# Rotary embedding on one core: a partition's DRAM run doubled from 16 KB to 32 KB, partitions interleaved from two batches

## The chip, the cores and the metric

The kernel runs on one core of a Trainium2 chip. The metric is the device time of one execution in microseconds (us). Runs are sorted into a fast and a slow state by time and granted clock; all timed runs quoted were in the fast state, and one single look has the state "unknown".

## The reference

```python
batch, seq, dim = (16, 512, 1024);  num_heads = 16      # head_dim 64, half 32
x1, x2 = x[..., :half_dim], x[..., half_dim:]           # per head
rotated = concatenate([x1 * cos - x2 * sin, x1 * sin + x2 * cos], axis=-1)   # cos, sin: [seq, 32]
```

Everything is float32. The input has 33.55 MB and so has the output. Each number is read once, used in two multiplications and an addition, and written once.

## The kernel before

A tile is one batch: 128 partitions with R = 4 rows each, 2 MB, and in DRAM one contiguous run of 16 KB for each partition. A ring of 40 rows (ten tiles) lives in SBUF, the core's on-chip memory. The sync engine's queue (SP) issues loads, the scalar engine's queue (ACT) issues stores. One row of a tile in all 128 partitions is a "unit" of work: VectorE multiplies by the cosines, GpSimd (for one unit in eight VectorE) multiplies the swapped halves by the sines, and VectorE, or TensorE with ScalarE, adds the two and writes back into the ring.

```python
R = 4;  RING = 40;  NC = batch
xv = x.rearrange("b (p r) d -> b p (r d)", r=R)
ov = out.rearrange("b (p r) h d -> b p (r h d)", r=R)

def on_sync(sp):
    for c in range(NC):
        if c * R >= RING:
            sp.wait_ge(sem_out[c - RING // R], 16)      # the slot's old tile has been stored
        sp.dma_start(tile(c), xv[c]).then_inc(sem_in[c], 16)
        if c == 0:
            ... # cos and sin tables: 128 partitions x 512 B each
# on_scalar, after the last unit of tile c:
    ae.dma_start(ov[c], tile(c)).then_inc(...)
```

Of the kernel before, what the change touches and what calls it, by code (L numbers as in the profile page):

```python
# [6 lines left out]
def bass_split_heads_rope_kernel(  # L7
# [14 lines left out]
    batch, seq, dim = x.shape  # L22
    H = int(num_heads)
    HD = dim // H
    HALF = HD // 2
    P = 128
    R = 4
    assert P * R == seq

    fp32 = mybir.dt.float32  # L30
    bf16 = mybir.dt.bfloat16
    mult = mybir.AluOpType.mult
# [1 line left out]
    COPY = mybir.ActivationFunctionType.Copy  # L34

    RING = 40
    NC = batch
    NU = batch * R

    def where(u):  # L40
        return u // R, u % R, u % RING


    PE2 = [u % 8 in (1, 3, 6) for u in range(NU)]
    V2 = [u % 8 == 3 for u in range(NU)]

    def count(flags):
        return [sum(flags[: u + 1]) for u in range(NU)]

    n_pool = count([not v for v in V2])  # L50
    n_dve = count(V2)
    n_pe = count(PE2)
# [3 lines left out]
    NT2 = 6  # L56
# [4 lines left out]
    with ExitStack() as stack:  # L61
        x_sb = stack.enter_context(nc.sbuf_tensor([P, RING, H, 2, HALF], fp32))
        t2_sb = stack.enter_context(nc.sbuf_tensor([P, NT2, H, 2, HALF], fp32))
        stage = stack.enter_context(nc.sbuf_tensor([P, 2, R * HALF], fp32))
        s_sb = stack.enter_context(nc.sbuf_tensor([P, R, 2, HALF], fp32))
        ident = stack.enter_context(nc.sbuf_tensor([P, P], fp32))
        zero = stack.enter_context(nc.sbuf_tensor([P, BANK], bf16))
        tab_ps = stack.enter_context(nc.psum_tensor([P, BANK], fp32))
        t1_ps = stack.enter_context(nc.psum_tensor([P, NT1, H * HD], fp32))
        sem_in = [stack.enter_context(nc.semaphore(f"in{c}")) for c in range(NC)]  # L70
        sem_out = [stack.enter_context(nc.semaphore(f"out{c}")) for c in range(NC - RING // R)]
        sem_rest = stack.enter_context(nc.semaphore("rest"))
        sem_cos = stack.enter_context(nc.semaphore("cos"))
        sem_sin = stack.enter_context(nc.semaphore("sin"))
        sem_c = stack.enter_context(nc.semaphore("ctab"))
# [9 lines left out]
        sem_a = stack.enter_context(nc.semaphore("act"))  # L85

        c_ps = tab_ps[:, 0:R * HALF].rearrange("p (r d) -> p r d", d=HALF)
        s_ps = tab_ps[:, R * HALF:R * (HALF + HD)].rearrange("p (r t d) -> p r t d", t=2, d=HALF)

        xv = x.rearrange("b (p r) d -> b p (r d)", r=R)  # L90
        ov = out.rearrange("b (p r) h d -> b p (r h d)", r=R)
        xs = x_sb[:].rearrange("p n h t d -> p n (h t d)")

        def tile(c):
            k = c * R % RING
            return x_sb[:, k:k + R].rearrange("p n h t d -> p (n h t d)")

        def swapped(k):
            return x_sb[:, k, :, ::-1, :]

        def sin_of(table, r):
            return table[:, r, None, :, :].broadcast_to([P, H, 2, HALF])

        def wait_added(eng, u):

            if n_pe[u]:
                eng.wait_ge(sem_a, n_pe[u])
            if n_comb[u]:
                eng.wait_ge(sem_v, n_comb[u])

        def wait_t2_free(eng, u):

            if u >= NT2:
                v = u - NT2
                if PE2[v]:
                    eng.wait_ge(sem_e, n_pe[v])  # L116
                else:
                    eng.wait_ge(sem_v, n_comb[v])

        def on_sync(sp):  # L120
            for c in range(NC):
                if c * R >= RING:
                    sp.wait_ge(sem_out[c - RING // R], 16)
                sp.dma_start(tile(c), xv[c]).then_inc(sem_in[c], 16)  # L124
                if c == 0:
                    for i, (table, sem) in enumerate(((cos, sem_cos), (sin, sem_sin))):
                        sp.dma_start(  # L127
                            stage[:, i, :], table.rearrange("(p r) d -> p (r d)", r=R)
                        ).then_inc(sem, 16)
            sp.wait_ge(sem_rest, 16 * (NC - len(sem_out)))  # L130

        def on_scalar(ae):
            ae.wait_ge(sem_sin, 16)
            sv = stage[:, 1, :].rearrange("s (r d) -> s r d", d=HALF)
            ae.activation(s_sb[:, :, 0, :], sv, COPY, scale=-1.0)  # L135
            ae.activation(s_sb[:, :, 1, :], sv, COPY).then_inc(sem_s, 1)  # L136
            for u in range(NU):
                c, r, k = where(u)
                if PE2[u]:
                    ae.wait_ge(sem_e, n_pe[u])  # L140
                    ae.activation(xs[:, k, :], t1_ps[:, u % NT1, :], COPY).then_inc(sem_a, 1)  # L141
                if r == R - 1:
                    wait_added(ae, u)
                    ae.dma_start(ov[c], tile(c)).then_inc(sem_out[c] if c < len(sem_out) else sem_rest, 16)

        def on_tensor(pe):
            pe.wait_ge(sem_z, 1)
# [5 lines left out]
            pe.wait_ge(sem_i, 2)  # L153
            for u in range(NU):
                if not PE2[u]:
                    continue
                pe.wait_ge(sem_m, u + 1)
                if V2[u]:
                    pe.wait_ge(sem_d, n_dve[u])
# [14 lines left out]
        def on_gpsimd(pl):  # L174
            pl.memset(ident[:], 1.0).then_inc(sem_i, 1)  # L175
            pl.wait_ge(sem_i, 1)
            pl.affine_select(  # L177
                out=ident[:],
                in_=ident[:],
                compare_op=mybir.AluOpType.is_equal,  # L180
                fill=0.0,
                base=0,
                pattern=[[-1, P]],
                channel_multiplier=1,
            ).then_inc(sem_i, 1)
            pl.wait_ge(sem_s, 1)
            for u in range(NU):
                if V2[u]:
                    continue
                c, r, k = where(u)  # L190
                pl.wait_ge(sem_in[c], 16)
                wait_t2_free(pl, u)
                pl.tensor_tensor(  # L193
                    t2_sb[:, u % NT2, :, :, :], swapped(k), sin_of(s_sb, r), mult
                ).then_inc(sem_p, 1)

        def on_vector(ve):
            ve.memset(zero[:], 0.0).then_inc(sem_z, 1)  # L198
            cv = stage[:, 0, :].rearrange("s (r d) -> s r d", d=HALF)
            sv = stage[:, 1, :].rearrange("s (r d) -> s r d", d=HALF)  # L200
            ve.wait_ge(sem_cos, 16)
            ve.tensor_copy(c_ps, cv)  # L202
            ve.wait_ge(sem_sin, 16)
            ve.tensor_scalar_mul(s_ps[:, :, 0, :], sv, -1.0)  # L204
            ve.tensor_copy(s_ps[:, :, 1, :], sv).then_inc(sem_c, 1)  # L205
            ve.wait_ge(sem_c, 1)
            ve.wait_ge(sem_w, NT1 * EH)

            def mul(u):
                c, r, k = where(u)  # L210
                if r == 0:
                    ve.wait_ge(sem_in[c], 16)
                if V2[u]:
                    wait_t2_free(ve, u)
                    ve.tensor_tensor(  # L215
                        t2_sb[:, u % NT2, :, :, :], swapped(k), sin_of(s_ps, r), mult
                    ).then_inc(sem_d, 1)
                if u >= NT1:
                    v = u - NT1
                    if PE2[v]:  # L220
                        ve.wait_ge(sem_a, n_pe[v])  # L221
                    else:
                        ve.wait_ge(sem_v, n_comb[v])  # L223
                ve.tensor_tensor(  # L224
                    t1_ps[:, u % NT1, :].rearrange("p (h d) -> p h d", d=HALF),
                    x_sb[:, k, :, :, :].rearrange("p h t d -> p (h t) d"),
                    c_ps[:, r, None, :].broadcast_to([P, 2 * H, HALF]),
                    mult,
                ).then_inc(sem_m, 1)

            def comb(u):
                c, r, k = where(u)
                ve.wait_ge(sem_m, u + 1)
                ve.wait_ge(sem_p, n_pool[u])  # L234
                ve.tensor_tensor(  # L235
                    xs[:, k, :],
                    t1_ps[:, u % NT1, :],
                    t2_sb[:, u % NT2, :, :, :].rearrange("p h t d -> p (h t d)"),
                    add,
                ).then_inc(sem_v, 1)  # L240

            for u in range(NU + LEAD):
                if u < NU:
                    mul(u)
                if u >= LEAD and not PE2[u - LEAD]:
                    comb(u - LEAD)

        on_sync(nc.sync)
        on_scalar(nc.scalar)
        on_gpsimd(nc.gpsimd)  # L250
        on_tensor(nc.tensor)
        on_vector(nc.vector)


# [31 lines left out]
```

## Time and profile before

| | before |
|---|---|
| median time | 162.06 us (3 runs, 162.05 to 162.24) |
| span of the profiled run | 160.5 us |
| VectorE, GpSimd busy | 82%, 81% |
| DMA queues q1 (loads), q10 (stores) | 49.9% + 48.8% of 16 engines' span |

The page of the kernel before: busy tenths in 40 slices, the rate, and the DMA queues with packets, megabytes and their share of the span of 16 DMA engines.

```profile
DVE  0089299999999879999999699998999799969400
POOL 1069999999999999999999993998939988498000
DMA  5999999999999999999999999999999999999996
GB/s 151 404 445 429 433 429 404 412 441 421 433 445 416 441 433 418 441 421 437 431 425 441 421 441 425 433 437 420 441 429 429 433 425 441 429 429 437 421 435 290
DMA packets 4899, 67.27 MB, mean 419 GB/s; under 512 B 544, under 2 KB 800, under 8 KB 800
q1 hardware_dynamic: 2592, 33.69, 49.9%
q10 hardware_dynamic: 2304, 33.56, 48.8%
```

The DMA row stays at 9 from the second slice to the last but one. The compute rows thin out at the end while DMA goes on. The DMA engines bound this kernel. The Trainium skill's page "DMA: Bandwidth & Descriptors", section "Where 436 GB/s comes from", derives a ceiling of 435.2 GB/s from 16 ports; the full slices of this trace sit at 404 to 445 GB/s, around 429 (the page counts a packet's bytes in the slice where it starts, so a slice can pass the ceiling). So only per-packet cost, the start and the end are left to win.

The timeline of the kernel before, first the SP queue from the start, then the first and the last store on the ACT queue (start us, duration us, what):

```profile
0.80 0.37 SPq L124 DMA_DIRECT2D x_sb<-in_x_dram  x1
1.22 0.42 SPq L127 DMA_DIRECT2D stage<-in_cos_dram  x1
1.70 0.42 SPq L127 DMA_DIRECT2D stage<-in_sin_dram  x1
...
22.09 0.38 ACTq L144 DMA_DIRECT2D out_dram<-x_sb  x1
...
150.47 0.34 ACTq L144 DMA_DIRECT2D out_dram<-x_sb  x1
```

The first load is issued at 0.80 us. The first store is issued at 22.09 us. The last load lands at 137.7 us; after that only stores move, and from the last store's issue at 150.47 us it takes another 10 us to the end.

**Packet records.** The trace also holds a record (start, length, bytes, queue) of each DMA packet. The kernel before has 4,096 data packets of 16,384 B, 256 per DMA engine, and their usual length is 611 ns. The records do not name the engine. I rebuilt the 16 sequences by following each packet to the next one that starts as it ends. On a rebuilt engine a packet starts about 4 ns (3 to 5) *before* the record of the packet ahead of it ends.

### The profile page before, as it was taken

The numbers are of one execution on the slowest core, as the hardware profiler recorded it, in microseconds if no ns is written. First come the engines' busy times: TensorE is split into PE (matmuls) and PEld (weight loads), VectorE is DVE, ScalarE is ACT, GpSimd is POOL, SyncE is SP. The second block draws the span as 40 slices with busy tenths as digits, with TensorE's granted clock in tenths as the row PEclk, the third lists the DMA queues.
The fourth block names the chain that finished last, engine by engine and source line by source line (L and its number), as shares of the span: only waits on it lengthen the run. The fifth ranks groups of instructions, "written<-read, shape, count | busy, mean of one in ns | idle before, by whom it ended". The sixth has DMA issues, their size and how long they took to land.

```text
span 160.5 us, 607 instructions
## 1 busy us (share of the span) xinstructions
PE 81.7 (51%) x102; PEld 25.4 (16%) x102; DVE 131.5 (82%) x116; ACT 26.3 (16%) x27; POOL 130.3 (81%) x62
## 2 busy tenths in 40 slices
PE   6004928354833944854573584575485436576000
PEld 1002402110210220211022021122022002112000
DVE  0089299999999879999999699998999799969400
ACT  3010221122022022012202202211211220220200
POOL 1069999999999999999999993998939988498000
PEclk9999996879595558595765555765567795567555
DMA  5999999999999999999999999999999999999996
GB/s 151 404 445 429 433 429 404 412 441 421 433 445 416 441 433 418 441 421 437 431 425 441 421 441 425 433 437 420 441 429 429 433 425 441 429 429 437 421 435 290
DMA packets 4899, 67.27 MB, mean 419 GB/s; under 512 B 544, under 2 KB 800, under 8 KB 800
## 3 DMA queue, kind: packets, MB, share of 16 engines
q1 hardware_dynamic: 2592, 33.69, 49.9%
q10 hardware_dynamic: 2304, 33.56, 48.8%
q14 instruction: 3, 0.02, 0.0%
HBM read 33.69 MB, written 33.55 MB: 419 GB/s over the span
## 4 chain that ended last, share of the span: by engine, by line
DVE 36%; PE 19%; issue 17%; POOL 10%; ACT 5%; DMA 5%; SPq 0%; DVEq 0%; POOLq 0%
PE t_ps L164 19%; DVE x_sb L235 18%; DVE t_ps L224 15%; POOL t_sb L193 10%; ACT x_sb L141 5%; DMA stage<-in_sin_dram 5%; DVE t_sb L215 4%; SPq L127 0%; SPq L124 0%; ACT s_sb L135 0%; ACT s_sb L136 0%; DVEq L234 0%; DVEq L223 0%; POOLq L116 0%; DVEq L221 0%
## 5 line engine op out<-in xcount | busy, mean ns | idle before, releaser
L193 POOL TENSOR_TENSOR t_sb<-x_sb,s_sb 128x1024 f32<-128x1024 f32 x56 | 129.6, 2376 | 17.0 <-DMA x_sb<-in_x_dram 8.9
L164 PE MATMUL t_ps<-t_sb,ident 128*128 128x512 f32 x96 | 78.9, 972 | 65.8 <-DVE t_ps L224 49.8
L224 DVE TENSOR_TENSOR t_ps<-x_sb,tab_ps 128x1024 f32<-128x1024 f32 x64 | 77.1, 1227 | 10.4 <-ACT x_sb L141 8.6
L235 DVE TENSOR_TENSOR x_sb<-t_ps,t_sb 128x1024 f32<-128x1024 f32 x40 | 48.6, 1217 | 0.0
L141 ACT ACTIVATE x_sb<-t_ps 128x1024 f32<-128x1024 f32 x24 | 24.6, 1023 | 115.8 <-PE t_ps L164 100.9
L164 PEld LDWEIGHTS t_ps<-t_sb,ident 128*128 128x128 f32 x96 | 24.7, 281 | 119.4 <-DVE t_ps L224 86.4
L215 DVE TENSOR_TENSOR t_sb<-x_sb,tab_ps 128x1024 f32<-128x1024 f32 x8 | 9.7, 1210 | 0.0
L202 DVE COPY tab_ps<-stage 128x128 f32<-128x128 f32 x1 | 0.3, 294 | 7.6 <-DMA stage<-in_cos_dram 7.6
L150 PE MATMUL t_ps<-zero 128*128 128x512 bf16 x6 | 2.7, 630 | 1.3 <-DVE zero L198 1.3
L135 ACT ACTIVATE s_sb<-stage 128x128 f32<-128x128 f32 x1 | 0.3, 309 | 6.9 <-DMA stage<-in_sin_dram 6.9
L135 ACT ACT_TABLE_LOAD x1 | 1.3, 1283 | 0.8 <-PEq L268 0.8
L150 PEld LDWEIGHTS t_ps<-zero 128*128 128x128 bf16 x6 | 0.7, 137 | 2.4 <-DVE zero L198 1.2
L198 DVE MEMSET zero<- 128x256 uint32 x1 | 0.3, 272 | 0.9 <-PEq L268 0.9
L175 POOL MEMSET ident<- 128x128 f32 x1 | 0.2, 204 | 0.3 <-POOLq L268 0.3
L177 POOL TENSOR_SCALAR_AFFINE_SELECT ident<-ident 128x128 f32<-128x128 f32 x1 | 0.3, 292 | 0.1
L268 POOL MEMSET const-float32-0.0<- 128x1 f32 x1 | 0.1, 98 | 0.3 <-issue 0.3
L136 ACT ACTIVATE s_sb<-stage 128x128 f32<-128x128 f32 x1 | 0.3, 293 | 0.0
L204 DVE TENSOR_SCALAR tab_ps<-stage 128x128 f32<-128x128 f32 x1 | 0.3, 283 | 0.0
L205 DVE COPY tab_ps<-stage 128x128 f32<-128x128 f32 x1 | 0.3, 283 | 0.0
L268 POOL MEMSET const-bfloat16-1.0<- 128x1 bf16 x1 | 0.1, 101 | 0.0
L268 POOL MEMSET const-uint8-127<- 128x1 uint8 x1 | 0.1, 101 | 0.0
L268 POOL MEMSET const-float32-1.0<- 128x1 f32 x1 | 0.1, 98 | 0.0
## 6 DMA issues: line engine op xcount, KB each, us to landing
x_sb<-in_x_dram SPq DMA_DIRECT2D x16, 2048.0 KB, 52.5
out_dram<-x_sb ACTq DMA_DIRECT2D x16, 2048.0 KB, 19.3
stage<-in_cos_dram SPq DMA_DIRECT2D x1, 64.0 KB, 7.5
stage<-in_sin_dram SPq DMA_DIRECT2D x1, 64.0 KB, 7.2
```

Of the source, the lines that this page charges most:

```text
L135: ae.activation(s_sb[:, :, 0, :], sv, COPY, scale=-1.0)
L136: ae.activation(s_sb[:, :, 1, :], sv, COPY).then_inc(sem_s, 1)
L141: ae.activation(xs[:, k, :], t1_ps[:, u % NT1, :], COPY).then_inc(sem_a, 1)
L150: pe.matmul(t1_ps[:, k, b * BANK:(b + 1) * BANK], zero[:, 0:P], zero[:], start=True, stop=True).then_inc(sem_w, 1)
L164: ins = pe.matmul(t1_ps[:, u % NT1, b * BANK:(b + 1) * BANK], ident[:], t2[:, b * BANK:(b + 1) * BANK], start=False, stop=True, skip_group ...
L177: pl.affine_select(out=ident[:], in_=ident[:], compare_op=mybir.AluOpType.is_equal, fill=0.0, base=0, pattern=[[-1, P]], channel_multiplier=1,
L193: pl.tensor_tensor(t2_sb[:, u % NT2, :, :, :], swapped(k), sin_of(s_sb, r), mult).then_inc(sem_p, 1)
L198: ve.memset(zero[:], 0.0).then_inc(sem_z, 1)
L215: ve.tensor_tensor(t2_sb[:, u % NT2, :, :, :], swapped(k), sin_of(s_ps, r), mult).then_inc(sem_d, 1)
L224: ve.tensor_tensor(t1_ps[:, u % NT1, :].rearrange("p (h d) -> p h d", d=HALF), x_sb[:, k, :, :, :].rearrange("p h t d -> p (h t) d"), c_ps ...
L235: ve.tensor_tensor(xs[:, k, :], t1_ps[:, u % NT1, :], t2_sb[:, u % NT2, :, :, :].rearrange("p h t d -> p (h t d)"), add,).then_inc(sem_v, 1)
L268: nc = _bacc.Bacc("TRN2", target_bir_lowering=False, num_devices=1)
```

## The change

The intent is fewer, larger descriptors (a descriptor is the order for one contiguous piece; each is a packet in the records): R = 8 rows, so 32 KB of DRAM for each partition. 128 x 8 rows are two batches, so partition 2s + b takes rows 8s to 8s + 7 of batch b of a pair. The ring is the same 20 MB, now five tiles of 4 MB. The first load and the last store go in two halves (2 MB, 16 KB per partition), so that compute starts as early as before and ends with a short store. The diff, cut to its core:

```diff
-    R = 4
+    R = 8
+    BL = P * R // seq          # 2 batches to a tile
+    SB = P // BL               # 64
+    G = batch // BL            # 8 tiles
+    loads = pieces(0)          # (tile, first row, rows); tile 0 in halves
+    stores = pieces(G - 1)     # last tile in halves
...
-        xv = x.rearrange("b (p r) d -> b p (r d)", r=R)
-        ov = out.rearrange("b (p r) h d -> b p (r h d)", r=R)
+        xv = x.rearrange("(g b) (s r) d -> g s b (r d)", b=BL, r=R)
+        ov = out.rearrange("(g b) (s r) h d -> g s b (r h d)", b=BL, r=R)
...
                         sp.dma_start(
-                            stage[:, i, :], table.rearrange("(p r) d -> p (r d)", r=R)
+                            stage[:, i, :],
+                            table.rearrange("(s r) d -> s (r d)", r=R)[:, None, :].broadcast_to([SB, BL, R * HALF]),
                         ).then_inc(sem, 16)
```

So the DRAM side of each transfer becomes *nested* (64 steps of 32 KB, and within each 2 steps of 2 MB), and the tables are 1 KB instead of 512 B in each partition. Compute is the same but for the copies of the tables.

## The prediction

> **What bounds the kernel now.** The 16 DMA engines, not arithmetic. The page's 40 slices show the DMA row at 9 tenths in all but the first and last slice, and 420 to 445 GB/s; the queue table gives the two transfer queues 49.9% and 48.8% of 16 engines' span, 98.7% together. In the packet records nearly every 16 KB packet, load or store, lasts 611 ns (loads average 622: the first ones, and some when stores begin, are slower). 16,384 B in 611 ns on 16 engines is 429 GB/s. The Trainium skill ("DMA: Bandwidth & Descriptors", section "Where 436 GB/s comes from") puts the ceiling at 435 GB/s, so at most 1.4% is left. VectorE (82% busy) and GpSimd (81%) follow behind: in the waits GpSimd idles 8.9 us for loads, and in the timeline the last store is issued at 150.5 us and lands about 10 us later, half of it queueing behind earlier stores.
>
> **What the change removes.** Packets. A 4 B packet lasts 9 ns, a 512 B one 27 ns, a 16 KB one 611 ns: a fixed 8 to 9 ns plus 0.0368 ns per byte. I estimate 1,214 ns for 32 KB, against 1,222 for two of 16 KB. Per engine 256 packets of 16 KB become 112 of 32 KB and 32 of 16 KB (first tile's load and last tile's store in halves): about 112 x 8.5 ns = 0.95 us less. Fourteen fewer completion packets per engine at 9 ns save 0.13 us.
>
> **What it adds.** Both tables go to 128 partitions as 1 KB, not 512 B: 16 packets per engine, about 19 ns longer each, +0.3 us of DMA time. The copies of the tables double in width (0.3 us each now), +0.2 to 0.5 us before the first tile is worked on, off the critical path because loads keep the DMA engines busy meanwhile. The instruction order shows VectorE and TensorE otherwise unchanged.
>
> **What it moves.** A tile takes 8 units of about 2.2 us, so the first store goes out at about 31 us, not 22.1. The five tiles in the ring (20 MB) need about 49 us to load alone, so the DMA engines do not starve. After that compute supplies 4 MB of stores per 17.6 us, more than half the DMA rate takes (19.5 us), so the store queue stays filled; loads keep about one tile queued when a slot is released. The loads end sooner (about 130 us, not 138). Compute should end no later than now (150 us), and the last half tile needs 4.9 us, so the DMA should still be busy when it is issued, with 3 to 5 us of room.
>
> **Address risk.** The skill (same page, "Latency and other measured facts", row pitch at powers of two) reports copies slowed at a 2 MB pitch. Here 2 MB separates only two batches[...]. I expect no effect; no run has shown it yet. If the nested source splits worse over the engines, packets would lengthen.
>
> **Sum.** 162.06 - 0.95 - 0.13 + 0.3 = about 161.3 us. Range 160.5 to 162.4. Faster by over 2%: 3%; within 2%: 89%; slower: 8%.
>
> **What would show it.** Packets fall from 4,899 to about 2,630; 32 KB packets last 1,210 to 1,216 ns for loads and stores alike; DMA stays at 9 tenths throughout; last load lands near 130 us; first store at 29 to 32 us; GpSimd's wait for loads after the first tile shrinks.
>
> **What would make it wrong.** 32 KB packets slower than twice 611 ns (addresses or ports); DMA gaps where load and store queues are both empty, from the coarser ring; a tail where the last half tile finds the engines idle.

## The result

| | before | changed |
|---|---|---|
| first comparison, median | 162.15 us (4 runs, 162.05 to 162.43) | 162.34 us (4 runs, 162.09 to 162.60) |
| ratio | | 1.0009 [0.9988, 1.0030] |
| control, five rounds, median | 161.90 us (11 runs) | 162.21 us (6 runs) |
| ratio | | 1.0019 [1.0005, 1.0033] |

A ratio is the mean time of one kernel's fast runs over the mean of the other's from the same rounds, so it is not quite the ratio of the medians shown. Brackets are 95% intervals. The forecast gain of 0.8 us did not come. The first comparison leaves open whether the change costs anything; in the control it costs 0.19%, which is 0.3 us.

The page of the changed kernel, the same rows as shown of before:

```profile
DVE  0079299998799999996999999996999899978500
POOL 1049999999999999999999899973999659995000
DMA  4999999999999999999999999999999999999995
GB/s 150 387 454 488 407 423 472 407 390 390 415 496 390 415 480 409 407 480 415 401 480 407 415 472 415 407 480 415 407 480 415 399 480 423 399 480 415 399 431 236
DMA packets 2882, 67.39 MB, mean 418 GB/s; under 512 B 320, under 2 KB 576, under 8 KB 576
q1 hardware_dynamic: 1584, 33.82, 49.6%
q10 hardware_dynamic: 1296, 33.56, 48.3%
```

The packets fell from 4,899 to 2,882 and the DMA row is as full as before. The queues' shares are 0.3 and 0.5 points lower, since 32 KB packets are a little shorter than two of 16 KB. The rate saws between about 390 and 500 GB/s as the 32 KB packets fall into one slice or the next. The timeline of the changed kernel, the lines that answer to those of before:

```profile
0.80 0.60 SPq L142 DMA_DIRECT2D x_sb<-in_x_dram  x1
1.46 0.59 SPq L145 DMA_DIRECT2D stage<-in_cos_dram  x1
2.10 0.60 SPq L145 DMA_DIRECT2D stage<-in_sin_dram  x1
...
31.64 0.62 ACTq L165 DMA_DIRECT2D out_dram<-x_sb  x1
...
151.46 0.55 ACTq L165 DMA_DIRECT2D out_dram<-x_sb  x1
```

The issues of all loads, before and then changed (shortest, median and longest in ns):

```profile
L124 SPq DMA_DIRECT2D x_sb<-in_x_dram x16: 327/446/1881, 0.8 to 86.2; - x16
L142 SPq DMA_DIRECT2D x_sb<-in_x_dram x9: 535/607/629, 0.8 to 95.2; - x9
```

Every issue of a nested transfer takes 0.54 to 0.63 us. Before, the first load takes 0.37 us and a store 0.34 to 0.38. By the packet records the first packet starts at 2.22 us instead of 1.80.

**A ledger of the DMA engines.** From the packet records I put each rebuilt engine's time into six parts and averaged over 16 engines. "Usual" is the packets at their usual length, less 5 ns for the overlap (16 KB: 606 ns, 32 KB: 1,208 ns, a table packet of 512 B: 22, of 1 KB: 41; a completion packet, 4 B, one for each transfer and engine: 4). "Gaps" is time between packets, counted from there; where the overlap is 4 ns, the missing 1 ns falls in here. "Stretch" is what packets took over their usual length: in the first 20 us, around the first store (20 to 40 us), and later. Microseconds; the parts sum to the mean end. The labels are those of the runs below.

| trace | first packet, mean | usual | gaps | stretch, start | stretch, first store | stretch, later | mean end | last engine's end |
|---|---|---|---|---|---|---|---|---|
| before | 2.06 | 155.62 | 0.43 | 0.89 | 0.42 | 0.10 | 159.52 | 160.17 |
| before_again | 2.02 | 155.62 | 0.47 | 0.91 | 0.40 | 0.10 | 159.53 | 160.16 |
| changed | 2.42 | 155.42 | 0.31 | 0.61 | 0.73 | 0.17 | 159.67 | 160.82 |
| after_again | 2.35 | 155.42 | 0.32 | 0.67 | 0.76 | 0.09 | 159.61 | 160.29 |
| e3_nested | 2.41 | 155.62 | 0.54 | 0.67 | 0.68 | 0.09 | 160.02 | 160.67 |
| e4_flat | 2.05 | 155.43 | 0.31 | 0.89 | 0.32 | 0.52 | 159.51 | 161.04 |
| e2_flat16k | 2.09 | 155.88 | 0.39 | 0.99 | 0.07 | 0.09 | 159.52 | 160.37 |
| e10_late_store | 2.18 | 155.62 | 0.47 | 0.75 | 0.25 | 0.10 | 159.37 | 160.07 |
| e11_tables512 | 2.39 | 155.12 | 0.29 | 0.62 | 0.94 | 0.09 | 159.46 | 160.33 |

Between before and the changed kernel (after_again, against the mean of both traces of before), usual time and gaps fall by 0.33 us. Against that stand a later first packet (+0.31), partly made up in the first 20 us (-0.23), and a larger stretch at the first store (+0.35). The mean end moves by +0.1 us. The kernel ends with the slowest engine, 0.13 to 0.65 us later than before in the two traces.

### The profile page after: what moved, and what is told of

Read it like the earlier page. It is cut to its first block, busy times and chain, and to the rows that moved or that the text cites. A ratio compares the mean times of both kernels' runs of the same rounds, so it can differ in the third digit from the quotient of the medians.

```text
span 161.2 us, 579 instructions
## 1 busy us (share of the span) xinstructions
PE 80.9 (50%) x102; PEld 24.8 (15%) x102; DVE 131.5 (82%) x116; ACT 26.6 (16%) x27; POOL 130.2 (81%) x62
## 2 busy tenths in 40 slices
DMA packets 2882, 67.39 MB, mean 418 GB/s; under 512 B 320, under 2 KB 576, under 8 KB 576
## 4 chain that ended last, share of the span: by engine, by line
DVE 39%; PE 20%; issue 17%; POOL 6%; ACT 6%; DMA 4%; SPq 1%; DVEq 0%; POOLq 0%
DVE x_sb L258 20%; PE t_ps L187 20%; DVE t_ps L247 15%; POOL t_sb L216 6%; ACT x_sb L161 5%; DMA stage<-in_sin_dram 4%; DVE t_sb L238 4%; SPq L142 0%; SPq L145 0%; ACT s_sb L154 0%; ACT s_sb L155 0%; DVEq L246 0%; DVEq L257 0%; DVEq L244 0%; POOLq L134 0%
## 5 line engine op out<-in xcount | busy, mean ns | idle before, releaser
L216 POOL TENSOR_TENSOR t_sb<-x_sb,s_sb 128x1024 f32<-128x1024 f32 x56 | 129.5, 2369 | 16.2 <-ACT s_sb L155 8.8
L187 PEld LDWEIGHTS t_ps<-t_sb,ident 128*128 128x128 f32 x96 | 24.0, 275 | 120.8 <-DVE t_ps L247 88.0
L154 ACT ACTIVATE s_sb<-stage 128x256 f32<-128x256 f32 x1 | 0.4, 416 | 7.2 <-DMA stage<-in_sin_dram 7.2
L155 ACT ACTIVATE s_sb<-stage 128x256 f32<-128x256 f32 x1 | 0.4, 399 | 0.0
```

Source lines behind the costliest of these rows:

```text
L154: ae.activation(s_sb[:, :, 0, :], sv, COPY, scale=-1.0)
L155: ae.activation(s_sb[:, :, 1, :], sv, COPY).then_inc(sem_s, 1)
L187: ins = pe.matmul(t1_ps[:, u % NT1, b * BANK:(b + 1) * BANK], ident[:], t2[:, b * BANK:(b + 1) * BANK], start=False, stop=True, skip_group ...
L216: pl.tensor_tensor(t2_sb[:, u % NT2, :, :, :], swapped(k), over_heads(s_sb[:, r]), mult).then_inc(sem_p, 1)
```

## The experiments

After the result I held this theory: (1) the fixed cost of a packet is nearer 5 ns than the 8.5 ns I used, because I read it from the length of records that overlap; (2) the nested pattern delays the start and enlarges the stretch at the first store. The rivals were the 8.5 ns of the prediction with a steady-state loss from two batches side by side; the size of packets (not the pattern) as the cause of the stretch; and the coarse 4 MB tiles.

### Packet count alone: e1_pad4k

The ring's row slots get 32 B of padding, so that no two rows of a partition are one run in SBUF and each row becomes a packet of its own.

```diff
-        x_sb = ...sbuf_tensor([P, RING, H, 2, HALF], fp32)
+        x_pad = ...sbuf_tensor([P, RING, H * HD + 8], fp32)
+        x_sb = x_pad[:, :, 0:H * HD].rearrange("p n (h t d) -> p n h t d", h=H, t=2)
-        xv = x.rearrange("b (p r) d -> b p (r d)", r=R)
+        xv = x.rearrange("b (p r) d -> b p r d", r=R)      # out in the same way
```

> The kernel before with 4 KB instead of 16 KB packets: 8 unused elements after each 4 KB ring slot, so that no two slots of a partition are one run; same DMA issues, same instructions, same bytes, 1024 data packets per engine, not 256. Theory of the prediction (8.5 ns fixed per packet): 768 x 8.5 ns = 6.5 us longer, about 168.7 us. Corrected theory (the record of a packet overlaps the next one's by about 5 ns, so only 4 to 5.4 ns are really spent per packet): 3.1 to 4.1 us longer, 165.2 to 166.3 us.

Measured: 166.06 us against 161.97 us, ratio 1.0252 [1.0239, 1.0265]. The page of e1_pad4k shows the same bytes in more packets:

```profile
DMA packets 17187, 67.27 MB, mean 408 GB/s; under 512 B 544, under 2 KB 800, under 8 KB 17184
q1 hardware_dynamic: 8736, 33.69, 50.5%
q10 hardware_dynamic: 8448, 33.56, 49.6%
```

17,187 less 4,899 packets on 16 engines are 768 more per engine; 4.09 us / 768 = 5.3 ns each. That is an upper figure, because the padding did one thing more than was meant: the first load is issued more slowly, and the first packet starts at 2.21 us, not 1.80 (on average over the engines 0.43 us later).

```profile
0.80 0.62 SPq L126 DMA_DIRECT2D x_pad<-in_x_dram  x1
```

In the records usual time and gaps grow by 3.7 us per engine, which is 4.8 ns a packet (3.3 ns usual time, 1.5 ns gaps). The 8.5 ns of the prediction would have made 6.5 us and is out. At 4.8 ns, 112 merged pairs per engine are worth 0.54 us, not 0.95. The Trainium skill ("DMA: Bandwidth & Descriptors", section "Why small descriptors are slow (HBM only)") states a fixed overhead of about 3 cycles per packet, an estimated 3.5 ns at the 850 MHz of the same page. It points the right way, and the measured 4.8 ns decides.

### The nested pattern alone: e3_nested

This is the kernel before with neighbouring partitions taken from the two halves of one batch. Packets, tiles and table bytes stay.

```diff
-        xv = x.rearrange("b (p r) d -> b p (r d)", r=R)
-        ov = out.rearrange("b (p r) h d -> b p (r h d)", r=R)
+        xv = x.rearrange("b (i s r) d -> b s i (r d)", i=2, r=R)
+        ov = out.rearrange("b (i s r) h d -> b s i (r h d)", i=2, r=R)
-   stage[:, i, :], table.rearrange("(p r) d -> p (r d)", r=R)
+   stage[:, i, :], table.rearrange("(i s r) d -> s i (r d)", i=2, r=R)
```

> The kernel before with neighbouring partitions taken from the two halves of one batch (1 MB apart), so that the DRAM side of every transfer is nested as in the changed kernel; packets stay 16 KB, tiles 2 MB, tables 512 B. If the nested pattern delays the first transfer: the first issue on the sync engine's queue lasts 0.6 us, not 0.37, the first packet starts near 2.2 us, not 1.8, and the time is 0.1 to 0.4 us longer than before. If not: 1.8 us and the same time within 0.1 us. The stretch at the first store stays near 0.4 us per engine if it goes by packet size, and becomes 0.7 if it goes by the pattern of addresses.

Measured: 162.45 us against 161.97 us, ratio 1.0032 [1.0019, 1.0044], so 0.5 us longer. The timeline of its SP queue at the start:

```profile
0.80 0.59 SPq L124 DMA_DIRECT2D x_sb<-in_x_dram  x1
1.45 0.59 SPq L127 DMA_DIRECT2D stage<-in_cos_dram  x1
2.08 0.60 SPq L127 DMA_DIRECT2D stage<-in_sin_dram  x1
```

The issue takes 0.59 us as in the changed kernel, and the first packet starts at 2.17 us. In the ledger the mean end is 0.5 us later: first packet +0.37, made up by 0.23 in the first 20 us; first store +0.27; gaps +0.09. The packets in steady state last 611 ns as before. So the pattern costs at the start of the loads and of the stores, not by a slower stream, and the stretch goes by pattern: all five traces with a nested main pattern (these four and e8 below) lie at 0.68 to 0.94 us, whether packets are 16 or 32 KB. A slow issue alone does not do it: in e2_flat16k below, with a plain pattern, the first store's issue also takes 0.61 us, and the stretch is 0.07 us. The stretched load packets are not those of the moment of issue but those in flight around the first store packet, which starts 3.5 to 3.9 us after its issue in the eight traces with a plain pattern (before: issue 22.09, first packet 25.83) and 4.3 to 5.1 us in the five nested ones (changed: 31.64 and 35.91). What there makes a load packet last up to 0.6 us longer on most engines, no run shows. The halves lie 1 MB apart here and the batches of the changed kernel 2 MB; no run varies the distance alone.

### A plain pattern with 32 KB and with 16 KB: e4_flat and e2_flat16k

In e4_flat partitions 0 to 63 take the first batch of a pair and 64 to 127 the second. The 4 MB are then one run, and each table is loaded by two transfers to 64 partitions.

```diff
-        xv = x.rearrange("(g b) (s r) d -> g s b (r d)", b=BL, r=R)
+        xv = x.rearrange("(g b) (s r) d -> g (b s) (r d)", b=BL, r=R)      # out in the same way
+   for b in range(BL):
+       sp.dma_start(stage[b * SB:(b + 1) * SB, i, :], table.rearrange("(s r) d -> s (r d)", r=R))
```

> The changed kernel with a plain pattern: partitions 0 to 63 from the first batch of a group, 64 to 127 from the second (a 4 MB run), tables loaded to each half by a transfer of its own; 32 KB packets, 4 MB tiles and halves as in the changed kernel. If the nested pattern costs the late start: first packet near 1.8 us and 0.1 to 0.4 us less than the changed kernel, about 162.0 us. If two batches side by side cost something in steady state, the excess of load packets after the first store also falls; I expect it not to. The stretch at the first store stays near 0.7 us per engine if packet size causes it.

e2_flat16k is e4_flat with 32 B of padding between the halves of each ring tile, which splits each 32 KB packet into two of 16 KB:

```diff
+        x_pad = ...sbuf_tensor([P, RING // 4, 4 * H * HD + 8], fp32)
+        xv = x.rearrange("(g b) (s q r) d -> g (b s) q (r d)", b=BL, q=2, r=R // 2)
```

> The flat kernel of the run e4_flat with 16 KB packets again (8 unused elements between the halves of each ring tile), all else as there: undoes the packet size alone. Prediction's theory: 112 x 8.5 = 0.95 us longer than e4_flat. Corrected theory: 112 x 4 to 5.4 ns = 0.45 to 0.6 us longer from the packets, but the load packets caught by the first store are stretched by about 0.4 us per engine as in the kernel before, not 0.7 as in the changed one, so net 0.1 to 0.3 us longer. If the stretch at the first store belongs to the later start of stores or to the 4 MB tiles and not to packet size, it stays 0.7 us and the net is 0.45 to 0.6.

Measured: e4_flat 162.81 us, ratio 1.0057 [1.0034, 1.0079]; e2_flat16k 162.13 us, ratio 1.0008 [0.9995, 1.0021]; both against 161.97 us. Both expectations missed. The larger packets made the flat kernel 0.7 us *slower*, where either theory had them save. The ledger shows how. From e2_flat16k to e4_flat usual time and gaps fall by 0.53 us, which is 4.7 ns for each of 112 pairs and agrees with the 4.8 ns of e1_pad4k. But the stretch at the first store is 0.25 us larger and the later stretch 0.43 larger, so the mean end does not move. And the later stretch is uneven: in e4_flat the engines end between 158.70 and 161.04 us, in e2_flat16k between 159.19 and 160.37. The kernel waits for the last. The stretched packets of e4_flat are mostly loads and come in bursts about every 20 us, near 54, 73, 93 and 113 us, where one 4 MB store ends and the next begins. That is where they are, not why; the cause stays open. The first packet did start at 1.80 us in both. Since e2_flat16k has the 4 MB tiles and the same time as before within its interval, the coarse ring in itself costs nothing that shows.

### One direction in 16 KB: e6_store16k and e7_load16k

These are e4_flat with all stores, or all loads, in two transfers of half the rows.

```diff
e6:  stores = [(g, r, R // 2) for g in range(G) for r in (0, R // 2)]   # with two store semaphores per ring slot
e7:  loads  = [(g, r, R // 2) for g in range(G) for r in (0, R // 2)]
```

> The kernel of e4_flat with every store in two transfers of 16 KB to a partition (so also finer stores), loads still 32 KB. If the stretched load packets and the 2.3 us spread of the engines' ends in e4_flat come from 32 KB store packets: the excess after 40 us falls from 0.4 to about 0.1 us per engine, the spread to about 1.2 us, and the time to 162.0 to 162.3 us. If they come from 32 KB load packets: as e4_flat, 162.6 to 163.

> The kernel of e4_flat with every load in two transfers of 16 KB to a partition, stores still 32 KB but for the last. The mirror of e6_store16k: 162.0 to 162.3 us if 32 KB load packets cause the stretch and the spread, as e4_flat if 32 KB store packets do; both improve if it takes both.

Measured, against 161.90 us: e6_store16k 163.72 us, ratio 1.0106 [1.0093, 1.0119]; e7_load16k 165.11 us, ratio 1.0199 [1.0181, 1.0217]. Both are worse than e4_flat, which neither alternative had. The edit changed more than I meant. The issue tables of e7_load16k, then of e6_store16k (KB of a transfer and median us from issue to landing):

```profile
x_sb<-in_x_dram SPq DMA_DIRECT2D x16, 2048.0 KB, 41.2
out_dram<-x_sb ACTq DMA_DIRECT2D x7, 4096.0 KB, 19.2
```

```profile
out_dram<-x_sb ACTq DMA_DIRECT2D x16, 2048.0 KB, 29.8
x_sb<-in_x_dram SPq DMA_DIRECT2D x7, 4096.0 KB, 26.5
```

A 4 MB store lands in 19.2 us in e7_load16k, and a store half as large needs 29.8 us in e6_store16k. The packet records say why. Between 40 and 50 us, e6_store16k starts 93 load packets and 89 store packets, so loads, with packets twice as large, get 68% of the bytes; e7_load16k starts 85 and 82, and loads get 34%; before starts 131 and 135, 49%. So in these runs the engines take about as many packets from one queue as from the other, whatever their size. The Trainium skill ("DMA: Bandwidth & Descriptors", section "Queues, rings and completion order") states such a round robin by packets. In e7_load16k the last load therefore lands at 143.7 us, not 129.5 as in e4_flat, the last store is issued at 155.95 us instead of 152.32, and most of the rebuilt engines stand idle for 0.7 to 1.5 us, from about 155.5 to 156.9 us. That is part of e7's loss: per engine the gaps are 1.0 us longer than in e4_flat, and the stretch after 40 us is 1.1 us larger (1.63 against 0.52), which stays unexplained. For e6_store16k no idle time shows; its later stretch is 0.87 us and its engines end between 159.54 and 161.97 us. Which direction caused the uneven stretch of e4_flat, these runs therefore do not tell.

### The changed kernel again, and its first load alone: after_again and e8_plain_first

> The changed kernel unaltered, as the control beside the other runs of this call and for a second trace. If the first comparison holds: 0.1 to 0.5 us longer than before. In the trace: first packet near 2.2 us, mean excess of load packets after 40 us of about 0.1 us per engine, and an instruction-fetch packet near 62 us on the engine that ends last.

after_again is the control quoted under the result: 162.21 us, ratio 1.0019 [1.0005, 1.0033]. First packet (2.18 us), stretch and the packet of instruction fetch (at 65.0 us) came as expected.

In e8_plain_first only the first load is issued differently, as one plain transfer for each batch, to every second partition.

```diff
+   if c == 0:
+       for b in range(BL):
+           sp.dma_start(tile(g, r, n)[b::BL], part(xv, g, r, n)[:, b]).then_inc(sem_in[c], 16)
```

> The changed kernel with only its first load issued as two plain transfers, one per batch, to every second partition; all else nested as before. If the late first packet (2.2 us, not 1.8) costs the changed kernel time: first packet near 1.8 us, 0.2 to 0.4 us less than after_again. If the start does not matter because the first packets only move a wait: same as after_again within 0.1 us.

Measured: 162.57 us, ratio 1.0042 [1.0025, 1.0058]. The edit did not do what it was for. The timeline of its SP queue:

```profile
0.80 1.18 SPq L144 DMA_DIRECT2D x_sb<-in_x_dram  x2
```

Each of the two issues takes 0.59 us, and the first packet starts at 2.12 us, hardly earlier. That need not be the stepping over SBUF partitions: in e4_flat the plain loads of the tables to 64 adjacent partitions take 0.53 to 0.60 us to issue as well. This run neither supports nor refutes the cost of the late start.

### The tables alone: e11_tables512

The changed kernel loads only half of each table row and uses it twice. Its output is wrong, which doesn't matter for the time.

```diff
-   stage[:, i, :], table...[:, None, :].broadcast_to([SB, BL, R * HALF])
+   stage[:, i, 0:RT * HALF], table...[:, None, 0:RT * HALF].broadcast_to([SB, BL, RT * HALF])      # RT = R // 2
```

> The changed kernel with half of each table loaded (512 B to a partition, not 1 KB) and used twice, wrong on purpose for rows 4 to 7 of a partition: takes away the tables' extra bytes alone. If they cost what their packets last (16 packets per engine, 19 ns each): 0.3 us less than the changed kernel, so about as before, within 0.1 us. If they are hidden at the start: as the changed kernel, 0.2 to 0.4 us over before.

Measured: 162.02 us, ratio 1.0001 [0.9987, 1.0015], against 161.98 us of before. Usual time falls by 0.30 us from the changed kernel, to the 10 ns what the table packets last. The mean end falls by less, 0.15 to 0.21 us, because the stretch at the first store was larger here (0.94 us). In time, 1.0001 here against 1.0019 of the changed kernel fits 0.3 us, but the intervals overlap. So the DMA time of the wider tables is as the prediction said, and the time of the kernel does not contradict it; it does not prove it alone.

### A later first store, and a second look at before: e10_late_store and before_again

The kernel before, with the first store held back and issued together with the second:

```diff
+   for k in {0: (), 1: (0, 1)}.get(c, (c,)):
+       ae.dma_start(ov[k], tile(k))...
```

> The kernel before with the first store held back until the second tile is done, then both issued together; nothing else. Load packets caught by the first store were stretched by 0.42 us per engine before and by 0.07 in e2_flat16k, whose first store goes out at 32 us and not 22. If the later start is why: the stretch falls to about 0.1 us and the time by 0.2 to 0.4 us, a version that beats both. If the addresses are why: the stretch stays near 0.4 us and the time is as before within 0.1 us.

Measured: 161.94 us, ratio 1.0000 [0.9988, 1.0012]. The stretch at the first store was 0.25 us, between the two alternatives, and the time did not move. It is no version that beats both; none of these runs is.

> The kernel before unaltered, for a second trace: first packet near 1.8 us, stretch of load packets at the first store near 0.4 us per engine, an instruction-fetch packet near 62 us on the engine that ends last.

161.93 us. Its ledger repeats that of before to within 0.04 us in each part, which says how far the parts of the ledger repeat. Which engine ends last depends on how the 16 sequences are rebuilt and is less sure.

## Why the prediction was wrong

The time lay inside the stated range, but the forecast was a gain of 0.8 us, and the medians show a loss of 0.2 and 0.3 us, clear of noise in the second comparison only.

- **"A fixed 8 to 9 ns" per packet: the mis-sized term of the sum.** The lengths were right (1,214 ns predicted for 32 KB, 1,213 measured), and so was their difference of 9 ns from two of 16 KB. What failed was taking the record's length for the engine's time. The next packet starts about 4 ns before the record ends, so each packet less gives that overlap up again, and 5 of the 9 ns are left. From start to start, 32 KB packets follow each other at 1,209 ns (median) and 16 KB packets at 607, twice which is 1,214. e1_pad4k gives 4.8 ns. The removal is 0.54 us for 112 packets and an estimated 0.07 for 14 completion packets, not 0.95 and 0.13.
- **"+0.3 us" for the tables: right as DMA time.** e11_tables512 takes it away and gets 0.30 us of usual time back; the kernel's time agrees, within its noise.
- **"Address risk ... I expect no effect": the step that failed outright.** Nested pairs of partitions cost 0.5 us in e3_nested, without 32 KB packets, 4 MB tiles or wider tables. I looked for it in the length of steady packets, which is unchanged. It sits in a slower issue (0.60 us, first packet at 2.2 us) and in a larger stretch when stores begin (0.7 us, not 0.4). The slow rates at large pitches in the skill's section "Latency and other measured facts", which I had named as the risk, do not show here: with halves 1 MB and batches 2 MB apart, packets keep their length.
- **The ring, the overlap and the tail: mostly right.** The DMA engines never starve; the first store goes out at 31.6 us (29 to 32 predicted) and the last load lands at 129.3 us (about 130). Compute ends a little later, not "no later": the last store is issued at 151.5 us, not 150.5, with no idle DMA engine after it. GpSimd's wait for loads shrank from 8.9 to 7.5 us, and in the second traces from 6.4 to 3.3. The packet count was 2,882 and not 2,630 because I had left out most of the 320 small packets, the completions.

Put together from the runs: +0.52 (nested) - 0.54 - 0.07 (packets) + 0.30 (tables) = +0.21 us. The two comparisons of the changed kernel show 0.0009 and 0.0019 of 162 us, +0.15 and +0.3 us. The sum takes its terms as independent, and that is not shown: on the flat pattern the same merging of packets lost 0.7 us (e2_flat16k to e4_flat) instead of saving 0.5. That the sum comes out may so be luck in part. The small rest, and which engine ends last, vary from run to run and are not settled. Nor is the uneven stretch of the flat kernel with 32 KB packets, which is why the pattern's cost cannot simply be taken away: e4_flat, without nesting, is slower than the changed kernel.

## What to carry to other kernels

When the DMA engines are bound and packets already have 16 KB, a packet less is worth about 5 ns, under 1% of its time; price it by how often packets *start*, or by padding a layout to make more of them, and not by the length of a record. A larger run that needs a nested access pattern or duplicated table bytes easily costs more than that, at the start of the first load and of the first store, where a steady-state rate does not show it. Keep load and store packets the same size: here the engines shared by packets, so the stream with smaller ones got about a third of the bytes, and both such kernels were slower.

## What the Trainium skill lacked or had wrong

- "DMA: Bandwidth & Descriptors", section "Why small descriptors are slow (HBM only)": it calls joining descriptors into packets worth it only up to 256 B a descriptor. With 4 KB packets instead of 16 KB the fixed cost was 3.7 us of 166 here, 4.8 ns a packet, against an estimated 3.5 ns from its 3 cycles at 850 MHz.
- The same page, section "Queues, rings and completion order": it speaks of draining 9 to 17 descriptors typically before changing queues. With descriptors of 16 or 32 KB the records of the two queues came about one for one (93 to 89, 131 to 135), and with unequal sizes the larger got 66 to 68% of the bytes.
- The same page, section "Latency and other measured facts": it gives a first byte at about 600 ns and does not say from when. For a plain first load the first packet came 0.63 us after the end of the issue and 1.0 us after its start (0.80 to 1.17, first packet at 1.80), for a nested one 0.8 and 1.4 us; for the first store, behind queued loads, it came 3.7 us after the start of the issue in the kernel before and 4.3 us in the changed one. That a transfer with a nested DRAM side, with padded SBUF rows or to 64 partitions takes about 0.6 instead of 0.37 us to issue I found on no page.
- "Runtime: NRT & Kernel Launch", section "Instruction fetch mechanics", has instructions fetched through a DMA queue of their own and the cost mostly hidden; what such a packet does to the data packets of a kernel bound by DMA I found on no page. Each trace has two or three of 8 KB and 309 ns (once 314) while the kernel runs, near 62 and 78 us and in some near 155 us. The first of them was followed by a load packet of 0.53 to 0.66 us over its length (in e1_pad4k by two packets, 0.23 and 0.33 us). In both traces of the changed kernel the (rebuilt) engine that ends last is one with such a packet; over the 13 traces it is nine by my rebuild and six and eight by two others with other rules of matching. This was seen, not tested.
- No page that I read says that the first store stretches the load packets in flight: 0.07 to 0.94 us per engine in these traces.
